# Row factors only in a gated delta rule's preparation, and a norm weight folded into the output weights

## The chip, the cores and the metric

The kernel runs on one core of one Trainium2 chip. The metric is the time of one execution in device microseconds (us); the median of three runs is shown. Engines are named as in the profile: PE is TensorE (matrix products), PEld its weight loads, DVE is VectorE, ACT is ScalarE, POOL is GpSimd, SP is SyncE, whose queue issues most DMAs.

## The reference, cut to what matters

One layer of a decoder trunk on 1040 positions (16 learned meta tokens and 1024 real ones) of width 1024: RMSNorm, one input projection, a gated-DeltaNet group of 4 heads (128 wide) beside a forgetting-attention group of 8 heads (64 wide), one output projection, a SwiGLU feed-forward part, a final norm. The change lies in the DeltaNet group:

```python
q = l2norm(q) * DK ** -0.5;  k = l2norm(k)          # x * rsqrt(sum(x*x) + EPS), per token
gc = cumsum(g)                                       # log decay inside a chunk
a_mat = strict(k @ k.T * exp(gc_i - gc_j) * beta_i)  # strictly lower triangular
u, w = solve(I + a_mat, [v * beta, k * beta * exp(gc)])
# scan over the chunks, with state s:
v_new = u - w @ s
o     = (q * exp(gc)) @ s + (q @ k.T * decay) @ v_new
s     = s * exp(g_last) + (k * exp(g_last - gc)).T @ v_new
# output of the group
o = o * rsqrt(mean(o * o) + EPS) * norm_w * silu(z)
```

`norm_w` (`gdn_norm_w`) has 128 numbers, one per column of a head, the same for all heads. The group's output then meets the rows of `w_out`.

## The kernel before, in words

All large products run in fp32r with three products per pair: each operand is split into a high part (an ACT cast, line 163) and a low part (a DVE difference, line 164). The helper `split` issues both; `load_w` (line 167) loads a block of weights into a raw tile and splits it, in `parts_n[0]` parts.

**First stage** (to about 50 us): for each of 8 blocks of 128 tokens the norm, transposes, and a projection that gives half of the gate z and the decay columns. `gate_out` (line 298) takes silu of z on ACT, multiplies it by the norm weight on POOL (line 302, the weight broadcast to all partitions in `gnw`), and writes it to a record in DRAM, `rec_d`. The other half of z comes later in `fox()`, through the same helper.

**Preparation of the recurrence** (to about 262 us): two pairs of heads. For a pair, k, q and v are projected (`conv_silu`, lines 418 to 429; a causal convolution on DVE), then `gdn_pre` (line 444) runs for each of the two heads. It

- transposes k, squares it and sums (`stat`), does the same for q, and takes the power -1/2 of both on POOL (lines 463 and 464: `rk`, `rq`);
- brings `rk` from a column (one number per token on its partition) into a row that every partition can read: two PE transposes (466, 467), two DVE copies, two DMA writes to `rk_d`, one broadcast read into `rkr` (474);
- loads the row of `gc`, forms the decay `e` and a strictly masked copy `na` (lines 479 to 488; `gcr` and `e` are two halves of one tile `gce`, one exponential for both, two masks on POOL);
- multiplies the products k k^T and k q^T from PSUM (`pq`, line 493) by the decay and the row factors (498, 500), and `na` by the column factor `rkr` on POOL (502);
- writes `na`, the decayed q k^T, k, v, and q to the record (lines 503 to 518), and handles the 16 meta tokens (520 to 526).

The tiles of squares (`sq`) are used again for the transposed values (`vtok`, line 509). `mkv`, the meta tokens' k and v, has two buffers.

`invert_blocks` (line 537) inverts the 32x32 diagonal blocks of `na` on DVE, in a chain of 31 steps of two small instructions (533 and 535). After the second pair, a small inversion of the meta block (`amt`) follows in the same way.

**The merge** (`levels`, line 597, once per pair) puts the inverted blocks together to 64 and 128 on PE. Its loads and copies (601 to 610) come ahead of its first yield, its PE work after it. **The scan** (`chunk`) then runs over 8 chunks, and `fox()` projects the attention group's parts beside both. The out-projection (`wout_block`, `wout_gdn`) starts under the attention.

**What sets the order.** Up to the end of the preparation a planner orders the instructions of every engine by a timeline that it simulates; on the chip each engine then takes its instructions in that order. From `levels` on, the PE order is written out by hand: `PeOrder` counts a time of its own, and chains with due times (`LV0` = 76 and 119 for the two merges) interrupt a filling stream of projections. The other engines stay with the planner. A tile of a pool that is allocated again waits for those that read it; in the pool `ubp` this goes by whole tiles. `issue_after` puts an instruction behind another on the same engine, without a semaphore.

Of the kernel before, what the change touches and what calls it, by code (L numbers as in the profile page):

```python
# [9 lines left out]
F32 = mybir.dt.float32  # L10
# [87 lines left out]
def tile_hymba_layer(ctx, tc, x, meta, attn_norm_w, w_in, conv_w, a_log, dt_bias, gdn_norm_w,  # L98
# [45 lines left out]
    rk_d = dram.tile([GH, T], F32, name="rk_d")  # L144
# [17 lines left out]
    def split(dst_hi, dst_lo, src):  # L162
        cast = nc.scalar.copy(dst_hi, src)  # L163
        tail[0] = (cast, nc.vector.tensor_sub(dst_lo, src, dst_hi.bitcast(F32)))  # L164
        return cast

    def load_w(parts, name, hl=None):
        n = sum(m for _, m in parts)
        raw = wraw.tile([P, WMAX], F32, tag="raw", name=f"raw_{name}")
        o = 0  # L170
        for src, m in parts:
            d = raw[:, o:o + m]
            if len(src.shape) == 3:
                d = d.rearrange("p (k c) -> p k c", k=src.shape[1])
            nc.sync.dma_start(d, src)
            o += m
        hi, lo = hl or (wsp.tile([P, WMAX], F32R, tag=f"w{c}", name=f"w{c}_{name}") for c in ("hi", "lo"))
        for a in range(0, n, n // parts_n[0]):
            b = min(n, a + n // parts_n[0])
            split(hi[:, a:b], lo[:, a:b], raw[:, a:b])  # L180
        return hi, lo
# [114 lines left out]
    gnw = gpool.tile([P, P], F32, name="gnw")  # L296

    def gate_out(t, acc, pool, tag, h0):
        zt = pool.tile([P, 4, 2, DH], F32, tag=tag, name=f"zt{h0}_{t}")
        zt = zt.rearrange("p a b c -> p (a b c)")[:, :256].rearrange("p (h c) -> p h c", h=2)  # L300
        nc.scalar.activation(zt, acc[:, :256].rearrange("p (h c) -> p h c", h=2), AF.Silu)
        nc.gpsimd.tensor_tensor(zt, zt, gnw[:, None, :].broadcast_to([P, 2, P]), op=ALU.mult)
        nc.sync.dma_start(rec_d[t, :, 7, h0:h0 + 2], zt)

    w = None
    for t in range(NT):
        load_norm(t)
        if w is None:
            w = win_block(GZ + 256, 264, "z1")
            nc.sync.dma_start(gnw, gdn_norm_w[0].partition_broadcast(P))  # L310
        acc = proj_tm(t, w, 0, 264, f"z1_{t}")
        nc.vector.tensor_copy(gt[:, t], acc[:, 256:264])
        gate_out(t, acc, zp, "zt", 2)
# [85 lines left out]
    cwr = gp.tile([P, P + NM], F32, tag="rkt", name="cwr")[:48, :P]  # L399
# [14 lines left out]
    rq = gpool.tile([P, GH, NT], F32, name="rq")  # L414
    rk = gpool.tile([P, GH, NS], F32, name="rk")
# [27 lines left out]

    def gdn_pre(h, kq, vt):
# [11 lines left out]
        mkv = gp.tile([NM, 2, P], F32, tag="mkv", bufs=2, name=f"mkv_{h}")  # L456
        nc.scalar.copy(mkv, pt[:NM, 0:2 * P].rearrange("p (a c) -> p a c", a=2))
# [4 lines left out]
        nc.vector.tensor_scalar(stat, stat, EPS, None, op0=ALU.add)
        nc.gpsimd.tensor_tensor(rk[:, h], stat[:, 0:NS], mhalf[:, :NS], op=ALU.pow)
        nc.gpsimd.tensor_tensor(rq[:, h], stat[:, NS:NS + NT], mhalf[:, :NT], op=ALU.pow)
        prk = ps_t(f"prk_{h}")
        nc.tensor.transpose(prk[:NT, :P], rk[:, h, 0:NT], ident)
        nc.tensor.transpose(prk[:1, P:P + NM], rk[:NM, h, NT:NS], ident[:NM, :NM])
        rkt = gp.tile([P, P + NM], F32, tag="rkt", name=f"rkt_{h}")[:NT]
        nc.vector.tensor_copy(rkt[:, :P], prk[:NT, :P])
        nc.vector.tensor_copy(rkt[:1, P:], prk[:1, P:P + NM])  # L470
        nc.sync.dma_start(rk_d[h, NM:T].rearrange("(t c) -> t c", c=P), rkt[:, :P])
        nc.sync.dma_start(rk_d[h:h + 1, 0:NM], rkt[:1, P:])
        rkr = gp.tile([P, T], F32, tag="rkr", name=f"rkr_{h}")
        nc.sync.dma_start(rkr, rk_d[h].partition_broadcast(P))
        nbr = gp.tile([P, NS], F32, tag="nbr", bufs=2, name=f"nbr_{h}")
        nc.vector.tensor_mul(nbr, nbeta[:, :, h], rk[:, h])
        nc.vector.tensor_mul(negc_[:, :, h], negc_[:, :, h], rk[:, h])

        gce = ubp.tile([P, 2, S], F32, tag="ul_p5", name=f"gce_{h}")
        gcr, e = v3(gce[:, 0]), v3(gce[:, 1])  # L480
# [3 lines left out]
        nc.scalar.activation(gce, gce, AF.Exp)  # L484
# [4 lines left out]
        for g in range(4):  # L489
            pq = ps_s(f"pq_{h}_{g}")  # L490
            for i in range(2):
                c = NM + P * (2 * g + i)
                nc.tensor.matmul(pq[:, 256 * i:256 * i + 256], kq[:, 0, c:c + P], kq[:, :, c:c + P],
                                 start=True, stop=True)
            pqv = pq.rearrange("p (i a c) -> p i a c", i=2, a=2)
            for i in range(2):
                t = 2 * g + i
                nc.vector.scalar_tensor_tensor(na[:, t], pqv[:, i, 0], nbr[:, t:t + 1], na[:, t],
                                               op0=ALU.mult, op1=ALU.mult)
                nc.vector.scalar_tensor_tensor(e[:, t], pqv[:, i, 1], rk[:, h, t:t + 1], e[:, t],  # L500
                                               op0=ALU.mult, op1=ALU.mult)
        nc.gpsimd.tensor_tensor(na, na, v3(rkr[:, NM:]), op=ALU.mult)
# [3 lines left out]
        kf = gp.tile([P, NT], F32, tag="kf", name=f"kf_{h}")  # L506
        nc.vector.tensor_mul(kf, rk[:, h, 0:NT], kdec[:, 0:NT, h])
        nc.gpsimd.tensor_tensor(ktok, ktok, kf[:, :, None].broadcast_to([P, NT, P]), op=ALU.mult)
        vtok = v3(sq)
# [12 lines left out]
        nc.vector.tensor_mul(ems[:, h], ems[:, h], rkr[:NM, :NM])  # L522
        nc.vector.scalar_tensor_tensor(nam[:, h], pm[:NM, :NM], nbr[:NM, NT:], ems[:, h], op0=ALU.mult, op1=ALU.mult)
        nc.vector.tensor_mul(kf[:NM, 0:1], rk[:NM, h, NT:NS], kdec[:NM, NT, h:h + 1])
        nc.vector.tensor_scalar(mkv[:, 0], mkv[:, 0], kf[:NM, 0:1], None, op0=ALU.mult)
# [70 lines left out]

    def levels(hp):
# [6 lines left out]
        V.transpose(tb.rearrange("p h t c -> p (h t c)"), ubk.rearrange("p h t c -> p (h t c)"))  # L604
        u = lp.tile([P, 2, NT, P], F32, tag="u", bufs=2, name=f"u_{hp}")
        nc.gpsimd.memset(u, 0.0)
        for b in range(4):
            r = slice(32 * b, 32 * b + 32)
            eng = nc.scalar.copy if b % 2 else V.tensor_copy
            eng(u[r, :, :, r], ubk[r])  # L610
# [41 lines left out]
        def up2_e(i, t0, p2):  # L652
            t2 = lp.tile([64, 2, 4, 64], F32, tag="t2", bufs=2, name=f"t2_{2 * hp + i}_{t0}")
            nc.scalar.copy(t2, p2[lo])
# [7 lines left out]
        def up3_e(i, t0, p3):  # L662
            h, ts = 2 * hp + i, slice(t0, t0 + 4)
            V.tensor_copy(u[lo, i, ts, hi], p3[lo, 0])
# [460 lines left out]
    def wout_block(k0, nb, tiles=None):  # L1125
        ws = ([], [])
        for i in range(2):
            hl = load_w([(wout_w(k0 + 2 * i, nb), 1024)], f"wo{k0}_{nb}{i}", tiles and tiles(i))
            for o, t in zip(ws, hl):
                o.extend(t[:, 512 * k:512 * k + 512] for k in range(2))  # L1130
# [6 lines left out]
    def wout_gdn(nb, tt):  # L1137
        if nb not in wvs:
            parts_n[0] = 2 if nb else 1
            wvs[nb] = wout_block(0, nb)  # L1140
# [547 lines left out]
```

## Time and profile before

| | |
|---|---|
| three runs, median (lowest to highest) | 1315.19 us (1314.64 to 1316.14) |
| profiled execution: time / span from first to last instruction | 1316.6 us / 1314.9 us |
| mean granted PE clock | 0.996 |
| PE / DVE / ACT / POOL busy | 1289.5 / 854.9 / 546.0 / 390.6 us |

A page of the profile gives, for each group of instructions, "line engine operation output<-inputs", its busy time and mean duration, and behind the second bar the idle time of the engine just before it with what ended that idle time. In a time line the brackets at the end of a row hold that idle time for the row alone. In the table of waits the three numbers are the total, the count and the longest. In the chain of waits (the work that ended last, followed back) a row "DMA x<-y" is a transfer that the next step waited for. Matrix products overlap, so PE busy time says where PE stood still rather than how much it does.

### The profile page before, as it was taken

The page shows a single profiled execution, that of the slowest core. Times are in us where ns is not written, and L with a number is a line of the kernel's source. Part 1 is how long each engine was busy: PE and PEld are TensorE (multiplying, and loading weights), DVE is VectorE, ACT ScalarE, POOL GpSimd, SP SyncE. Part 2 cuts the span into 40 slices and gives each one's busy share as a digit, 9 for nine tenths or more (in the row PEclk, how much of TensorE's full clock was granted, in tenths as well). Part 3 has the DMA queues.
Part 4 walks back from the last instruction along what each step waited for, and adds up shares of the span by engine and source line. Part 5 has one row for each costly group of instructions (what it writes and reads, how often), then busy time and mean ns, then how long its engine had stood idle before and what let it go on. Part 6 is the DMA issues. An engine that isn't in the chain of part 4 may idle for free.

```text
span 1314.9 us, 20026 instructions
## 1 busy us (share of the span) xinstructions
PE 1289.5 (98%) x7442; PEld 1128.9 (86%) x7442; DVE 854.9 (65%) x1526; ACT 546.0 (42%) x918; POOL 390.6 (30%) x347
## 2 busy tenths in 40 slices
PE   8999999999999999999999999999999999999998
PEld 8999999898999878887778888888888888888887
DVE  5665779677236768986897765556566565355545
ACT  5543434333223557885553332333323343343332
POOL 2211423601022321113432544554334453020301
PEclk9999999999999999999999999999999999999999
DMA  6331753774469886647434555534454557955523
GB/s 225 102 101 45 204 144 101 215 226 146 157 227 340 223 227 188 169 117 232 170 135 136 183 176 178 173 129 155 155 168 150 176 198 261 405 183 180 211 73 128
DMA packets 184360, 233.88 MB, mean 178 GB/s; under 512 B 19024, under 2 KB 136776, under 8 KB 181448
## 3 DMA queue, kind: packets, MB, share of 16 engines
q1 hardware_dynamic: 181368, 223.97, 52.9%
q0 software_dynamic: 2896, 8.65, 2.3%
q8 instruction: 58, 0.95, 0.3%
q14 instruction: 38, 0.31, 0.1%
HBM read 154.91 MB, written 77.67 MB: 177 GB/s over the span
## 4 chain that ended last, share of the span: by engine, by line
PE 74%; DVE 10%; DMA 7%; ACT 3%; issue 3%; SPq 1%; POOL 1%; POOLq 0%; DVEq 0%; ACTq 0%
PE xp L1569 9%; PE yp L1569 7%; PE gb L1403 5%; PE ud L1403 5%; PE ub L1403 5%; PE gd L1403 5%; PE ua L1403 4%; PE ga L1403 4%; PE pj_fq L207 3%; PE pj_fk L207 2%; PE ue L1403 2%; PE ge L1403 2%; PE wog L207 2%; PE pt L1034 2%; DVE up L533 1%
## 5 line engine op out<-in xcount | busy, mean ns | idle before, releaser
L164 DVE TENSOR_TENSOR al_p<-ra_p,ah_p 128x2048 fp32r<-128x2048 f32 (+1 forms) x21 | 45.7, 2175 | 94.9 <-ACT ah_p L163 94.9
L163 ACT CAST ah_p<-ra_p 128x2048 fp32r<-128x2048 f32 (+1 forms) x21 | 37.1, 1766 | 105.4 <-PE xp L1569 48.5
L1569 PE MATMUL xp<-wh_p,al_p 128*128 128x512 f32 (+1 forms) x176 | 67.3, 382 | 0.0
L1569 PE MATMUL xp<-wl_p,ah_p 128*128 128x512 f32 (+1 forms) x176 | 67.3, 382 | 0.0
L1569 PE MATMUL xp<-wh_p,ah_p 128*128 128x512 f32 (+1 forms) x176 | 67.3, 382 | 0.0
L1456 POOL TENSOR_TENSOR gzw<-gzw,uzt 128x512 f32<-128x512 f32 x11 | 18.4, 1676 | 153.5 <-DVE uzt L1447 127.3
L1456 POOL TENSOR_TENSOR gxy<-gxy,uxy 128x512 f32<-128x512 f32 x22 | 39.0, 1772 | 67.4 <-DVE uxy L1447 59.6
L1403 PE MATMUL gb<-uh_p,w_g_p 128*128 128x512 f32 x176 | 57.8, 389 | 0.0
L1403 PE MATMUL ub<-uh_p,w_u_p 128*128 128x512 f32 x176 | 57.7, 389 | 0.0
L1403 PE MATMUL ud<-uh_p,w_u_p 128*128 128x512 f32 x176 | 57.7, 389 | 0.0
L1403 PE MATMUL gd<-uh_p,w_g_p 128*128 128x512 f32 x176 | 57.7, 389 | 0.0
L164 DVE TENSOR_TENSOR w_u_p<-raw_u,w_u_p 128x512 fp32r<-128x512 f32 x42 | 43.0, 1023 | 21.6 <-ACT w_u_p L163 21.5
L163 ACT CAST ph<-pt 128x512 fp32r<-128x512 f32 (+1 forms) x96 | 45.1, 472 | 26.2 <-PE pt L1034 25.5
L1007 ACT ACTIVATE pr<-pr,sm 128x144 f32<-128x144 f32 (+3 forms) x64 | 50.5, 790 | 7.7 <-DVE sm L1002 7.3
L164 DVE TENSOR_TENSOR pl<-pt,ph 128x512 fp32r<-128x512 f32 (+1 forms) x96 | 51.4, 553 | 3.4 <-ACT ph L163 2.6
L1403 PE MATMUL ga<-uh_p,w_g_p 128*128 128x512 f32 x160 | 52.5, 389 | 0.0
L1403 PE MATMUL ua<-uh_p,w_u_p 128*128 128x512 f32 x160 | 52.5, 389 | 0.0
L1569 PE MATMUL yp<-wh_p,ah_p 128*128 128x512 f32 x132 | 51.3, 389 | 0.0
L1569 PE MATMUL yp<-wl_p,ah_p 128*128 128x512 f32 x132 | 51.3, 389 | 0.0
L1569 PE MATMUL yp<-wh_p,al_p 128*128 128x512 f32 x132 | 51.3, 389 | 0.0
L164 DVE TENSOR_TENSOR wl_p<-rw_p,wh_p 128x2048 fp32r<-128x2048 f32 (+1 forms) x21 | 46.9, 2236 | 3.4 <-ACT wh_p L163 3.4
L163 ACT CAST w_u_p<-raw_u 128x512 fp32r<-128x512 f32 x42 | 26.0, 620 | 53.1 <-PE gd L1403 34.1
(646 smaller groups left out, 4296.7 us busy)
## 6 DMA issues: line engine op xcount, KB each, us to landing
ra_p<-ao_p SPq DMA_DIRECT2D x14, 1024.0 KB
raw_g<-in_w_gate_dram SPq DMA_DIRECT2D x22, 512.0 KB
raw_u<-in_w_up_dram SPq DMA_DIRECT2D x22, 512.0 KB
raw_d<-in_w_down_dram SPq DMA_DIRECT2D x22, 512.0 KB
wt_p<-raw_d SPq DMA_DIRECT2D x33, 256.0 KB
rw_p<-wt_p SPq DMA_DIRECT2D x8, 1024.0 KB
rw_p<-in_w_down_dram SPq DMA_DIRECT2D x6, 1024.0 KB
ao_p<-gzw SPq DMA_DIRECT2D x22, 256.0 KB
```

Of the source, the lines that this page charges most:

```text
L163: cast = nc.scalar.copy(dst_hi, src)
L164: tail[0] = (cast, nc.vector.tensor_sub(dst_lo, src, dst_hi.bitcast(F32)))
L207: nc.tensor.matmul(dst, a, b, start=first, stop=last)
L533: V.tensor_tensor(pr[:, 0:m, 0:i + 1], u[:, 0:m, 0:i + 1], a[:, i:i + 1, 0:i + 1].broadcast_to([u.shape[0], m, i + 1]), op=ALU.mult)
L1007: nc.scalar.activation(pr[:, :n], pr[:, :n], AF.Exp, bias=sm[:, np_ - 1:np_], scale=-1.0, accum_out=rsum[:, h, j:j + 1])
L1034: nc.tensor.transpose(pt[:rows_k, P * j:P * j + P], pts[j][0][:, c0:c0 + rows_k], ident)
L1403: nc.tensor.matmul(dst, a[:, c], b[:, k], start=(first and k == 0 and i == 0), stop=(k == 3 and i == 2), skip_group_check=not first)
L1456: last_mul[0] = G.tensor_tensor(gs[d], gs[d], us[d], op=ALU.mult)
L1569: nc.tensor.matmul(dst[:, n_], a[:, f, c], b[:, f, n_], start=(first and i == 0 and n == 0), stop=(i == NF - 1 and n == 2), skip_group_che ...
```

## The change

The factor of k is taken out of the columns. With the matrix scaled by rows alone, its row factor becomes the square of the old one, that is the reciprocal of `stat` + EPS times -beta (`nbr`), computed on DVE right after k's squares and ahead of q's. The missing factors go elsewhere: `beta` is multiplied by `rk` in place (it is used after the merge, in `ub`), and k's record (`ktok`) and the meta tokens' k are scaled by the decay alone. `rk_d`, the transposes, the copies, the DMAs, `rkr` and `kf` fall away; the powers of k and q become one POOL call on a joint tile `rkq`; the decayed q k^T needs only the decay (four DVE products of 256 columns for eight of 128 with a factor).

Tiles: `gce` is allocated once for all heads, the decay `e` of odd heads gets a tile of its own (`eo`), the values one (`vtk`, which the convolution weights' load uses first), the exponential becomes two. `mkv` has one buffer. The second pair's DVE and ACT copies in `levels` are put behind the last ones of the first pair.

The norm weight no longer multiplies silu(z). It is loaded as one number per partition, and the splits of the output weights' DeltaNet rows are scaled by it: the high part as a scaled copy on ACT, the low part as a fused multiply and subtract on DVE (two blocks of 128 x 1024, then four of 128 x 512).

```diff
@@ -159,12 +158,18 @@
-    def split(dst_hi, dst_lo, src):
-        cast = nc.scalar.copy(dst_hi, src)
-        tail[0] = (cast, nc.vector.tensor_sub(dst_lo, src, dst_hi.bitcast(F32)))
+    def split(dst_hi, dst_lo, src, col=None):
+        if col is None:
+            cast = nc.scalar.copy(dst_hi, src)
+            low = nc.vector.tensor_sub(dst_lo, src, dst_hi.bitcast(F32))
+        else:
+            cast = nc.scalar.activation(dst_hi, src, AF.Copy, scale=col)
+            low = nc.vector.scalar_tensor_tensor(dst_lo, src, col, dst_hi.bitcast(F32),
+                                                 op0=ALU.mult, op1=ALU.subtract)
+        tail[0] = (cast, low)
         return cast
...
@@ -293,13 +298,12 @@
-    gnw = gpool.tile([P, P], F32, name="gnw")
+    gnw = gpool.tile([P, P], F32, name="gnw")[:, 0:1]
...
         nc.scalar.activation(zt, acc[:, :256].rearrange("p (h c) -> p h c", h=2), AF.Silu)
-        nc.gpsimd.tensor_tensor(zt, zt, gnw[:, None, :].broadcast_to([P, 2, P]), op=ALU.mult)
         nc.sync.dma_start(rec_d[t, :, 7, h0:h0 + 2], zt)
...
-            nc.sync.dma_start(gnw, gdn_norm_w[0].partition_broadcast(P))
+            nc.sync.dma_start(gnw, gdn_norm_w.rearrange("o p -> p o"))
...
@@ -411,8 +415,8 @@
-    rq = gpool.tile([P, GH, NT], F32, name="rq")
-    rk = gpool.tile([P, GH, NS], F32, name="rk")
+    rkq = gpool.tile([P, GH, NS + NT], F32, name="rkq")
+    rk, rq = rkq[:, :, 0:NS], rkq[:, :, NS:]
...
+    gce = ubp.tile([P, 2, S], F32, tag="ul_p5", name="gce")
+
     def gdn_pre(h, kq, vt):
...
-        mkv = gp.tile([NM, 2, P], F32, tag="mkv", bufs=2, name=f"mkv_{h}")
+        mkv = gp.tile([NM, 2, P], F32, tag="mkv", name=f"mkv_{h}")
...
+        nc.vector.tensor_scalar(stat[:, 0:NS], stat[:, 0:NS], EPS, None, op0=ALU.add)
+        nbr = gp.tile([P, NS], F32, tag="nbr", bufs=2, name=f"nbr_{h}")
+        nc.vector.reciprocal(nbr, stat[:, 0:NS])
+        nc.vector.tensor_mul(nbr, nbr, nbeta[:, :, h])
         for g, pt in enumerate(tr8(kq[:, 1], f"q{h}")):
             nc.scalar.activation(sqq[:, 512 * g:512 * g + 512], pt, AF.Square)
         nc.vector.tensor_reduce(stat[:, NS:NS + NT], v3(sqq), AX.X, ALU.add)
-        nc.vector.tensor_scalar(stat, stat, EPS, None, op0=ALU.add)
-        nc.gpsimd.tensor_tensor(rk[:, h], stat[:, 0:NS], mhalf[:, :NS], op=ALU.pow)
-        nc.gpsimd.tensor_tensor(rq[:, h], stat[:, NS:NS + NT], mhalf[:, :NT], op=ALU.pow)
-        prk = ps_t(f"prk_{h}")
-        nc.tensor.transpose(prk[:NT, :P], rk[:, h, 0:NT], ident)
-        nc.tensor.transpose(prk[:1, P:P + NM], rk[:NM, h, NT:NS], ident[:NM, :NM])
-        rkt = gp.tile([P, P + NM], F32, tag="rkt", name=f"rkt_{h}")[:NT]
-        nc.vector.tensor_copy(rkt[:, :P], prk[:NT, :P])
-        nc.vector.tensor_copy(rkt[:1, P:], prk[:1, P:P + NM])
-        nc.sync.dma_start(rk_d[h, NM:T].rearrange("(t c) -> t c", c=P), rkt[:, :P])
-        nc.sync.dma_start(rk_d[h:h + 1, 0:NM], rkt[:1, P:])
-        rkr = gp.tile([P, T], F32, tag="rkr", name=f"rkr_{h}")
-        nc.sync.dma_start(rkr, rk_d[h].partition_broadcast(P))
-        nbr = gp.tile([P, NS], F32, tag="nbr", bufs=2, name=f"nbr_{h}")
-        nc.vector.tensor_mul(nbr, nbeta[:, :, h], rk[:, h])
+        nc.vector.tensor_scalar(stat[:, NS:NS + NT], stat[:, NS:NS + NT], EPS, None, op0=ALU.add)
+        nc.gpsimd.tensor_tensor(rkq[:, h], stat[:, 0:NS + NT], mhalf[:, :NS + NT], op=ALU.pow)
         nc.vector.tensor_mul(negc_[:, :, h], negc_[:, :, h], rk[:, h])
-
-        gce = ubp.tile([P, 2, S], F32, tag="ul_p5", name=f"gce_{h}")
-        gcr, e = v3(gce[:, 0]), v3(gce[:, 1])
+        nc.vector.tensor_mul(beta[:, :, h], beta[:, :, h], rk[:, h])
+
+        gcr = v3(gce[:, 0])
+        e = v3(gp.tile([P, S], F32, tag="eo", name=f"e_{h}") if h % 2 else gce[:, 1])
...
-        nc.scalar.activation(gce, gce, AF.Exp)
+        nc.scalar.activation(e, e, AF.Exp)
+        nc.scalar.activation(gcr, gcr, AF.Exp)
...
-                nc.vector.scalar_tensor_tensor(e[:, t], pqv[:, i, 1], rk[:, h, t:t + 1], e[:, t],
-                                               op0=ALU.mult, op1=ALU.mult)
-        nc.gpsimd.tensor_tensor(na, na, v3(rkr[:, NM:]), op=ALU.mult)
+            ts = slice(2 * g, 2 * g + 2)
+            nc.vector.tensor_mul(e[:, ts], pqv[:, :, 1], e[:, ts])
...
-        kf = gp.tile([P, NT], F32, tag="kf", name=f"kf_{h}")
-        nc.vector.tensor_mul(kf, rk[:, h, 0:NT], kdec[:, 0:NT, h])
-        nc.gpsimd.tensor_tensor(ktok, ktok, kf[:, :, None].broadcast_to([P, NT, P]), op=ALU.mult)
-        vtok = v3(sq)
+        nc.gpsimd.tensor_tensor(ktok, ktok, kdec[:, 0:NT, h, None].broadcast_to([P, NT, P]), op=ALU.mult)
+        vtok = v3(gp.tile([P, S], F32, tag="vtk", name=f"vtk_{h}"))
...
-        nc.vector.tensor_mul(ems[:, h], ems[:, h], rkr[:NM, :NM])
...
-        nc.vector.tensor_mul(kf[:NM, 0:1], rk[:NM, h, NT:NS], kdec[:NM, NT, h:h + 1])
-        nc.vector.tensor_scalar(mkv[:, 0], mkv[:, 0], kf[:NM, 0:1], None, op0=ALU.mult)
+        nc.vector.tensor_scalar(mkv[:, 0], mkv[:, 0], kdec[:NM, NT, h:h + 1], None, op0=ALU.mult)
...
@@ -601,13 +597,15 @@ def levels(hp):
-        V.transpose(tb.rearrange("p h t c -> p (h t c)"), ubk.rearrange("p h t c -> p (h t c)"))
+        with tc.issue_after(lv_t["dve"].ins) if hp else nullcontext():
+            V.transpose(tb.rearrange("p h t c -> p (h t c)"), ubk.rearrange("p h t c -> p (h t c)"))
...
-            eng(u[r, :, :, r], ubk[r])
+            with tc.issue_after(lv_t["act" if b % 2 else "dve"].ins) if hp else nullcontext():
+                eng(u[r, :, :, r], ubk[r])
...
-            nc.scalar.copy(t2, p2[lo])
+            lv_t["act"] = nc.scalar.copy(t2, p2[lo])
...
-            V.tensor_copy(u[lo, i, ts, hi], p3[lo, 0])
+            lv_t["dve"] = V.tensor_copy(u[lo, i, ts, hi], p3[lo, 0])
...
-            wvs[nb] = wout_block(0, nb)
+            wvs[nb] = wout_block(0, nb, col=gnw)
```

More of the change, by code (lines that the diff above doesn't have):

```diff
@@ L143, in tile_hymba_layer @@
     gc_d = dram.tile([GH, S], F32, name="gc_d")
-    rk_d = dram.tile([GH, T], F32, name="rk_d")
     rec_d = dram.tile([NT, P, 8, GH, P], F32, name="rec_d")
@@ L160, in tile_hymba_layer, with load_w @@
     tail = [None]
-    def split(dst_hi, dst_lo, src):
-        cast = nc.scalar.copy(dst_hi, src)
-        tail[0] = (cast, nc.vector.tensor_sub(dst_lo, src, dst_hi.bitcast(F32)))
+    def split(dst_hi, dst_lo, src, col=None):
[7 more added lines that the diff above has]
+        tail[0] = (cast, low)
         return cast
-    def load_w(parts, name, hl=None):
+    def load_w(parts, name, hl=None, col=None):
         n = sum(m for _, m in parts)
@@ L179, in load_w @@
             b = min(n, a + n // parts_n[0])
-            split(hi[:, a:b], lo[:, a:b], raw[:, a:b])
+            split(hi[:, a:b], lo[:, a:b], raw[:, a:b], col)
         return hi, lo
@@ L398, in tile_hymba_layer @@
     gp = gpc.enter_context(tc.tile_pool(name="gp", bufs=1))
-    cwr = gp.tile([P, P + NM], F32, tag="rkt", name="cwr")[:48, :P]
+    cwr = gp.tile([P, S], F32, tag="vtk", name="cwr")[:48, :P]
     nc.sync.dma_start(cwr, conv_w.rearrange("i (m p) -> (i m) p", p=P))
@@ L595, in b3 @@
         return col[:, :, None].broadcast_to([col.shape[0], col.shape[1], P])
+    lv_t = {}
     def levels(hp):
@@ L1123, in tile_hymba_layer, with wout_block @@
     wvs = {}
-    def wout_block(k0, nb, tiles=None):
+    def wout_block(k0, nb, tiles=None, col=None):
         ws = ([], [])
         for i in range(2):
-            hl = load_w([(wout_w(k0 + 2 * i, nb), 1024)], f"wo{k0}_{nb}{i}", tiles and tiles(i))
+            hl = load_w([(wout_w(k0 + 2 * i, nb), 1024)], f"wo{k0}_{nb}{i}", tiles and tiles(i), col)
             for o, t in zip(ws, hl):
```

## The prediction

> **What bounds the kernel now.** I read the engine shares first, then the table of 20 us stretches, the waits of TensorE, and last the time lines and the chain of waits around each place where TensorE stood still.
>
> ```profile
> PE 1289.5 (98%) x7442; PEld 1128.9 (86%) x7442; DVE 854.9 (65%) x1526; ACT 546.0 (42%) x918; POOL 390.6 (30%) x347
> ...
> 160.00:180.00 20.00, 19.41 (x120) 18.92 (x119) 13.96 (x24) 7.11 (x9) 4.04 (x4) 1.00 0.77 205
> 180.00:200.00 20.00, 19.38 (x122) 19.10 (x121) 18.93 (x34) 7.27 (x9) 3.84 (x4) 1.00 0.31 90
> ...
> 220.00:240.00 20.00, 18.71 (x144) 16.71 (x142) 18.09 (x35) 8.58 (x15) 7.61 (x7) 1.00 0.68 199
> 240.00:260.00 20.00, 18.74 (x135) 18.10 (x136) 12.24 (x39) 4.61 (x8) 13.30 (x13) 0.91 0.77 210
> ...
> 300.00:320.00 20.00, 18.49 (x270) 16.59 (x269) 15.96 (x44) 5.89 (x11) 1.50 (x4) 1.00 0.52 147
> ```
>
> The columns are the stretch, its length, then the busy time of PE, PEld, DVE, ACT and POOL with counts, the granted clock, and DMA share and GB/s. TensorE is busy 98% of the span, so time taken off another engine is worth nothing by itself. A gain can come only from a TensorE instruction that is gone, from a stretch in which TensorE stood still, or from a stretch at a low clock. The recurrent preparation runs from about 118 to 262 us and its block inversions to about 320; in these rows TensorE idles 0.59 + 0.62 + 1.29 + 1.26 + 1.51 = 5.3 us, and one stretch has a clock of 0.91. The waits say who was late:
>
> ```profile
> PE prk L466 <- POOL rk L463: 2.1, 1, 2.1
> ...
> PE py L644 <- DVE u L634: 0.9, 2, 0.5
> ...
> PE pj_v L197 <- ACT cx_q L423: 0.6, 1, 0.6
> PE pq L493 <- DVE gce L500: 0.6, 1, 0.6
> PE py L644 <- ACT t L654: 0.6, 1, 0.6
> ...
> PE tr_q L437 <- ACT mkv L457: 0.4, 1, 0.4
> ```
>
> The change touches the chain behind every one of these rows.
>
> **The change part by part.**
>
> *The row transposes.* L466 and L467 and everything behind them go: two transposes, two copies, two small writes, one broadcast read and a POOL product per head.
>
> ```profile
> 132.01 0.27 PE L466 MATMUL prk<-ident,rk 128*8 128x128 f32 x1
> ...
> 132.31 1.09 PE L437 MATMUL tr_v<-ident,vt 128*128 128x128 f32 x8
> ...
> 241.26 0.27 PE L466 MATMUL prk<-ident,rk 128*8 128x128 f32 x1 [2.07 <-POOL rk L463]
> ```
>
> From 132.01 to 132.31 the pair takes 0.30 us of TensorE's time; four heads make **1.2 us**. The last row is head 3's pair, which waited 2.07 us for the powers on POOL. No TensorE instruction reads a power any more, so this wait has no successor of its own: **2.1 us**.
>
> *The clock behind that wait.*
>
> ```profile
> 239.00:241.00 2.00, 0.19 (x2) 0.00 (x0) 2.00 (x5) 0.06 (x1) 1.58 (x1) 1.00 0.46 146
> 241.00:242.50 1.50, 1.24 (x11) 1.09 (x11) 1.50 (x6) 1.41 (x1) 1.50 (x2) 1.00 0.51 66
> 242.50:246.00 3.50, 3.50 (x19) 3.26 (x18) 2.92 (x6) 1.71 (x4) 3.50 (x3) 0.53 0.35 47
> ...
> 14.00:17.00 3.00, 1.66 (x13) 1.20 (x11) 2.41 (x4) 1.78 (x6) 1.25 (x2) 1.00 0.71 235
> 17.00:21.00 4.00, 3.28 (x17) 3.13 (x16) 3.37 (x6) 1.74 (x4) 0.55 (x1) 0.57 0.80 264
> ```
>
> TensorE works 0.19 of 2 us from 239, and from 242.5 to 246 it is granted 0.53 of its clock. The other dip, from 17 to 21, also follows a stretch that was half idle (1.66 of 3). I take the dip for the gap's consequence: 3.5 x 0.47 = **1.6 us** that go with it. [...]
>
> *The queue waits of head 3 and of the first inversion.*
>
> ```profile
> 226.59 7.23 DMA rec_d<-gce
> 233.83 3.80 DMA gce<-gc_d
> ...
> 247.98 7.04 DMA rkr<-rk_d
> ...
> 314.05 0.62 ACT u L610
> ...
> 315.32 1.07 ACT t L654 x2
> ```
>
> ```profile
> L619 PE MATMUL py<-u,na x128: 191/191/212, 304.7 to 354.3; 32*32 32x32 f32 x128
> ...
> L502 POOL TENSOR_TENSOR ktna<-ktna,rkr 128x1024 f32<-128x1024 f32 x4 | 11.4, 2862 | 25.3 <-DVE ktna L498 9.9 <-DMA rkr<-rk_d 9.7 <-DVE kst L452 5.6
> ```
>
> In the chain of waits, head 3's decay load stands behind the write of head 2's `gce` (7.23 us), because both halves were one tile; with `e` of odd heads in its own tile that load waits only for the short-lived half. The factor's broadcast (7.04) and its product (2.86 a head) leave the chain altogether, so head 3's matrix reaches the second inversion 9 us earlier or more. TensorE uses that inversion's result only when the second merge starts, and the last products of that kind stand at 354.3, so this is no gain in itself; it takes DVE's inversion of the meta block (`amt`) away from the time of the first merge at 304.7. At 314 the second pair's copies of `ubk` stand in ACT's queue ahead of the first pair's `t`, for which TensorE waits; the change orders them behind it. The `py` waits are 0.9 + 0.6 = 1.5; I take **1.2**, as DVE's copy itself remains.
>
> *The smaller waits.*
>
> ```profile
> 184.12 1.92 ACT L484 ACTIVATE gce<-gce 128x2048 f32<-128x2048 f32 x1
> ...
> 228.62 1.06 ACT L451 ACTIVATE sq<-ktna 128x1024 f32<-128x1024 f32 x1 [4.10 <-DMA rec_d<-sq]
> 229.58 0.34 ACT L457 COPY mkv<-trm 16x256 f32<-16x256 f32 x1
> ```
>
> The copy that TensorE's `pj_v` waited for stood behind one exponential of 1.92 us; it becomes two of about half, the needed one first. `tr_q` waited behind a square that stood 4.10 us for the write of the shared value tile, and values now have their own. With the `pq` wait these are 0.6 + 0.4 + 0.6 = 1.6; the planner will place the copies anew, so I take half, **0.8**.
>
> *New waits.* `mkv` has one buffer, so L457 of heads 1 and 3 waits for the previous head's 16 KB write. Behind it on ACT stand the squares of q and the projection copies, and TensorE's `tr_q` waits for those. The write of head 2 is issued early:
>
> ```profile
> 224.85 1.17 SPq L526 DMA_DIRECT2D mkv_d<-mkv  x1
> ...
> 157.66 3.03 DMA rk_d<-rkt
> ```
>
> It has 4.7 us until L457 at 229.58, where a small write takes 3.03 to land, and it no longer waits for a power but only for the decay. Without that cover it would cost at most the difference, some 3 us. The write of the value tile has much longer. DVE gets a reciprocal, an addition and two products per head, each of at most 128x9 elements; they go into what the eight `e` products of 0.335 us, halved in number (next fence), and the two copies of the transposes leave free.
>
> *Work off the path.* The gate product and the factor's product leave POOL; the products of `e` on DVE become four instead of eight.
>
> ```profile
> L302 POOL TENSOR_TENSOR zt<-zt,gnw 128x256 f32<-128x256 f32 x16 | 15.4, 967 | 23.4 <-ACT zt L301 23.4
> ...
> L500 DVE SCALAR_TENSOR_TENSOR gce<-pq,rk,gce 128x128 f32<-128x128 f32 x32 | 10.6, 335 | 0.7 <-POOL gce L487 0.7
> ...
> 442.59 1.14 ACT L163 CAST whi_wo<-raw_wo 128x512 fp32r<-128x512 f32 x2 [0.55 <-PE pj_fq L207]
> ...
> 181.54 1.23 DVE L483 SCALAR_TENSOR_TENSOR gce<-gce 128x1024 f32<-128x1024 f32 x1
> 182.77 1.23 DVE L164 TENSOR_TENSOR wlo_z<-raw_z,whi_z 128x1024 fp32r<-128x1024 f32 x1
> ```
>
> That is 15.4 us of POOL, with the factor's 11.4 above, at 30% load: worth nothing but the room it gives. Four `e` products of 256 columns lie between 4 and 8 times 0.335 us, so DVE gains 0 to 1.3 us a head, not on TensorE's path. The norm weight moves into six splits of output weights. On DVE the fused form and the plain difference take the same 1.23 us at 128x1024; on ACT a cast of 512 columns takes 0.57. A scaled copy does not stand in the trace; between no difference and doubling it is 0 to 0.57 us a piece, and I take zero, as the squares of that size on ACT (1.06 at 1024 columns, above) cost no more. The new load of the weight, one number a partition, has 400 us.
>
> *The sum.* 1.2 + 2.1 + 1.6 + 1.2 + 0.8 = 6.9. Against it I set 1.0 for waits that a new plan brings: the bounds are zero and 2.1, the longest that the old plan had here, and no row is nearer to one than the other. Net **5.9**. The profiled execution took 1316.6 us around a span of 1314.9; it becomes 1310.7. It stood 1.4 above the median of the three runs, 1315.19, so the median becomes **1309.3**.
>
> **The rivals.** *The waits only move* (no change). If what follows the transposes in TensorE's order was as late as they were, the 2.1 us and the dip stay, and only the transposes and part of the merge come back: 1.2 + 0.7 = 1.9, 1313.3. For it speaks that DVE was busy without a break from 239 to 242.5 and the value transposes stand right behind. Against it: those need only a finished value tile and a free bank, and the wait's row names the power alone.
>
> *The powers in front of the masks* (slower). POOL takes its work in order, and the masks L485 and L487 are what the `pq` products wait for.
>
> ```profile
> 239.41 1.79 POOL L463 TENSOR_TENSOR rk<-kst,mhalf 128x9 f32<-128x9 f32 x1 [4.20 <-DVE kst L462]
> 241.17 2.54 POOL L464 TENSOR_TENSOR rq<-kst,mhalf 128x8 f32<-128x8 f32 x1
> ...
> 247.92 1.09 POOL L485 TENSOR_SCALAR_AFFINE_SELECT ktna<-gce 128x1024 f32<-128x1024 f32 x1
> ```
>
> The powers become one call of about 1.79 + 2.54 = 4.3 us. Since the products no longer wait for a power, the planner may put `pq` earlier; if it counts the power as short, both `sp` banks fill and TensorE stands for power and mask, 4.3 + 1.1 = 5.4 us, and then loses 1.6 by the clock. In heads 1 and 3 that makes 14.0; less the 6.9 gained, the kernel ends at 1322.3. It turns the result from 6.9 us of new idling on. Against it: the same two powers stood ahead of the masks before, and `pq` waited 0.6 us once.
>
> *More than the sum.* If the room on POOL and DVE also shortens the starting stretch and its dip at 17 us (1.7) and the remaining small waits (0.8), and no new wait comes, it is 6.9 + 2.5 = 9.4: 1305.8.
>
> **How the numbers follow.** A difference of 0.2%, 2.6 us, is about what a measurement of this kernel can tell from none. The chances are 0.58 for the forecast, 0.22 for waits that only move, 0.12 for the powers in front of the masks, 0.08 for more. Faster by over 0.2% means below 1312.6: nearly all of the forecast (0.55), all of the last case and a quarter of the moved waits, 0.68. Within 0.2% are the rest of these two, 0.20; slower the third, 0.12. The forecast's own range is 1306.5 to 1312.5: the waits all gone and none new, or half of them gone. With the neighbours it reaches from 1305.0, under the last case, to 1316.5, which leaves out the slower case and little else.
>
> **What would show it.** In the changed profile the rows of `prk`, `rkt` and `rkr` are gone and no row of TensorE's waits names a power. The stretch from 240 to 260 has a clock of 1.00; if TensorE waits there under another name, the second case holds. `gce<-gc_d` no longer follows a write of `gce` by zero, and ACT's `u` copies of the second pair stand behind all `t` copies of the first. A wait of `pq` on POOL's masks above 2 us means the slower case. A wait of ACT's `mkv` on `mkv_d` would make the single buffer wrong. What I cannot see is the new plan as a whole: all rows past 320 us should be as they were, and if they are not, the sum is incomplete.

## The result, and the profile after

The changed kernel takes 1308.06 us (median of 4 runs, 1307.08 to 1308.18) beside 1315.32 us (1314.64 to 1316.14) for the kernel before in the same comparison: a ratio of 0.9941, 95% interval 0.9929 to 0.9954. The forecast was 1309.3. Its profiled execution took 1308.2 us around a span of 1306.5; before these were 1316.6 and 1314.9. The spans differ by 8.4 us, the medians by 7.3.

The stages show where. The next two fences give, for the kernel before and for the changed one, the last product of four kinds. The rows list shortest, median and longest duration in ns, then the first and the last start in us.

```profile
L199 PE MATMUL zg<-whi_z,ul x8: 167/168/169, 46.2 to 47.7; 128*16 128x8 f32 x8
...
L199 PE MATMUL pj_v<-uh,wlo_gv x96: 314/322/326, 94.8 to 201.6; 128*128 128x346 f32 x64, 128*128 128x348 f32 x32
...
L207 PE MATMUL fv<-whi_fv,ul x128: 274/282/425, 242.8 to 294.8; 128*128 128x264 f32 x64, 128*128 128x256 f32 x64
...
L207 PE MATMUL pj_fk<-uh,wlo_fk x96: 315/322/429, 295.2 to 350.1; 128*128 128x346 f32 x64, 128*128 128x348 f32 x32
```

```profile
L204 PE MATMUL zg<-whi_z,ul x8: 167/168/169, 43.6 to 45.0; 128*16 128x8 f32 x8
...
L204 PE MATMUL pj_v<-uh,wlo_gv x96: 315/322/326, 92.1 to 196.4; 128*128 128x346 f32 x64, 128*128 128x348 f32 x32
...
L212 PE MATMUL fv<-whi_fv,ul x128: 274/283/425, 235.7 to 288.9; 128*128 128x264 f32 x64, 128*128 128x256 f32 x64
...
L212 PE MATMUL pj_fk<-uh,wlo_fk x96: 315/322/434, 289.3 to 342.2; 128*128 128x346 f32 x64, 128*128 128x348 f32 x32
```

| stage, up to its last product | before | after | gained so far | in the stage |
|---|---|---|---|---|
| first stage (`zg`) | 47.7 | 45.0 | 2.7 | 2.7 |
| heads 0 and 1 (`pj_v`) | 201.6 | 196.4 | 5.2 | 2.5 |
| heads 2 and 3, value projections (`fv`) | 294.8 | 288.9 | 5.9 | 0.7 |
| both pairs' first part of the merge (`pj_fk`) | 350.1 | 342.2 | 7.9 | 2.0 |
| the rest, to the end of the span | 1314.9 | 1306.5 | 8.4 | 0.5 |

The forecast had nothing for the first row and 3.7 us (2.1 + 1.6) for the third. The table of stretches of the changed kernel, with the columns of the prediction's table, says why the third is small:

```profile
0.00:20.00 20.00, 16.86 (x111) 15.59 (x112) 10.83 (x16) 11.53 (x20) 5.36 (x21) 1.00 0.85 293
...
14.00:17.00 3.00, 1.74 (x14) 1.53 (x15) 2.56 (x5) 1.76 (x3) 0.89 (x1) 1.00 0.69 233
17.00:21.00 4.00, 4.00 (x35) 4.00 (x35) 3.24 (x7) 2.74 (x7) 0.55 (x1) 1.00 0.77 262
...
160.00:180.00 20.00, 20.00 (x128) 20.00 (x127) 16.89 (x40) 7.66 (x12) 0.10 (x1) 1.00 0.43 128
180.00:200.00 20.00, 20.00 (x130) 19.73 (x129) 19.79 (x28) 11.01 (x16) 3.30 (x3) 1.00 0.16 48
...
220.00:240.00 20.00, 20.00 (x160) 19.07 (x159) 6.85 (x19) 3.52 (x6) 6.76 (x8) 1.00 0.85 214
240.00:260.00 20.00, 17.00 (x127) 16.82 (x126) 14.54 (x60) 3.73 (x9) 1.28 (x2) 0.91 0.84 237
...
300.00:320.00 20.00, 20.00 (x231) 18.72 (x232) 8.24 (x13) 7.43 (x13) 4.30 (x4) 1.00 0.33 108
```

Of the five stretches of the prediction's table in which TensorE idled, four are now full. The fifth is worse: from 240 to 260 TensorE stands for 3.0 us, and the clock is 0.91 as before. In the waits of TensorE no row names a power any more, but a new row heads the list:

```profile
PE fv L212 <- DVE up L527: 3.0, 1, 3.0
```

It lies between the products that start at 241.14 and 244.43, within a value projection (`fv`) of the attention group. The time lines of ACT, DVE and SP in the changed kernel show the chain behind it, one fence each (a row SPq is the issue of a DMA in SP's queue):

```profile
241.33 0.36 ACT L163 CAST fvt_-1_2741<-fv_-1_2716 16x256 fp32r<-16x256 f32 x1 [7.23 <-DMA rec_d<-zt]
```

```profile
242.32 0.71 DVE L601 STREAM_TRANSPOSE tb<-ubk 128x512 f32<-128x512 f32 x1 [6.97 <-DMA ubk<-ud_d]
...
243.79 0.41 DVE L164 TENSOR_TENSOR fvt_-1_2741<-fv_-1_2716,fvt_-1_2741 16x256 fp32r<-16x256 f32 x1
```

```profile
229.70 1.92 SPq L502 DMA_DIRECT2D ad_d<-ktna  x4
231.66 0.45 SPq L509 DMA_DIRECT2D rec_d<-ktna  x1
232.21 0.53 SPq L510 DMA_DIRECT2D rec_d<-e  x1
232.96 2.58 SPq L537 DMA_DIRECT2D ad<-ad_d  x2
235.58 1.13 SPq L307 DMA_DIRECT2D rec_d<-zt  x2
237.56 0.32 SPq L597 DMA_DIRECT2D ubk<-ud_d  x1
...
240.50 2.70 SPq L599 DMA_DIRECT2D na<-rec_d  x2
```

The split of the first value block frees the PSUM bank that TensorE needs; the wait's row names `up` only because the inversion's first product starts right behind it on DVE, at 244.21. The cast of that split needs a tile slot that a gate tile held until its record write landed; its difference on DVE stands behind copies that waited for `ubk`. Both transfers had stood in SP's queue behind head 3's matrix (`ad_d`, `rec_d<-ktna`, `ad`).

### The profile page after: what moved, and what is told of

The parts are those of the page before. It is cut to its first block, busy times and chain, and to the rows that moved or that the text cites. A ratio compares the mean times of both kernels' runs of the same rounds, so it can differ in the third digit from the quotient of the medians.

```text
span 1306.5 us, 19943 instructions
## 1 busy us (share of the span) xinstructions
PE 1284.0 (98%) x7434; PEld 1127.0 (86%) x7434; DVE 847.0 (65%) x1502; ACT 549.3 (42%) x924; POOL 360.5 (28%) x323
## 4 chain that ended last, share of the span: by engine, by line
PE 85%; DVE 6%; ACT 3%; DMA 3%; issue 2%; SPq 1%; POOL 0%; POOLq 0%; DVEq 0%; ACTq 0%
PE xp L1567 9%; PE yp L1567 7%; PE gb L1401 5%; PE ud L1401 5%; PE gd L1401 5%; PE ub L1401 5%; PE ua L1401 4%; PE ga L1401 4%; PE pj_fk L212 4%; PE pj_fq L212 3%; PE fv L212 3%; PE ue L1401 2%; PE ge L1401 2%; PE pt L1032 2%; PE wog L212 2%
## 5 line engine op out<-in xcount | busy, mean ns | idle before, releaser
L164 DVE TENSOR_TENSOR al_p<-ra_p,ah_p 128x2048 fp32r<-128x2048 f32 (+1 forms) x21 | 46.7, 2222 | 94.5 <-ACT ah_p L163 94.5
L164 DVE TENSOR_TENSOR w_u_p<-raw_u,w_u_p 128x512 fp32r<-128x512 f32 x42 | 42.9, 1022 | 21.7 <-ACT w_u_p L163 21.5
L1454 POOL TENSOR_TENSOR gxy<-gxy,uxy 128x512 f32<-128x512 f32 x22 | 38.9, 1768 | 65.3 <-DVE uxy L1445 54.3
```

The lines of the kernel that those rows point to most:

```text
L164: low = nc.vector.tensor_sub(dst_lo, src, dst_hi.bitcast(F32))
L1454: last_mul[0] = G.tensor_tensor(gs[d], gs[d], us[d], op=ALU.mult)
```

## The experiments

Each comparison has its own runs of the kernel before on its chip; their medians were 1315.3 for the changed kernel and 1317.5 to 1318.0 for the runs below, so ratios are given beside times. The changed kernel was not run again beside them; mult_back and no_order, whose edits touch nothing that TensorE waits for in the changed kernel, came to 1308.2 and 1308.8, so on their chips the times bear a comparison with 1308.1 to within 1 us. Times of one stage come from the profiles, one of each kernel.

### The two halves apart: norm_only, rows_only

```diff
# norm_only: the kernel before with the norm weight moved: one column loaded, no product on POOL, scaled splits
...
+            cast = nc.scalar.activation(dst_hi, src, AF.Copy, scale=col)
...
-        nc.gpsimd.tensor_tensor(zt, zt, gnw[:, None, :].broadcast_to([P, 2, P]), op=ALU.mult)
...
# rows_only: the changed kernel with all of this undone
```

> The kernel before with only the norm weight moved (one column loaded, no product on POOL, scaled splits of the output weights); the recurrent preparation is the old one. Theory A, the start belongs to the norm weight: the first stage ends 2.7 us earlier than before and has no dip of the clock at 17 us, the wait of TensorE for the power at 240 us stays (2.1 us), total 1315.3 - 2.7 = 1312.6. Theory B, the forecast's (room on POOL, worth nothing): the first stage as before, 1315.3.

> The changed kernel without the move of the norm weight (broadcast load, product on POOL and plain splits again). Theory A: the start as before with its dip at 17 us, the rest as in the changed kernel, 1308.1 + 2.7 = 1310.8. Theory B (the start's gain comes from elsewhere, the order of the loads or the tiles): the start as in the changed kernel, 1308.1.

norm_only takes 1321.6 us beside 1317.5, a ratio of 1.0027 (1.0014 to 1.0041): slower. rows_only takes 1313.1, 0.9967 (0.9954 to 0.9980). The start goes the way that theory A says, though not to its end: the first stage of norm_only ends at 45.3, that of rows_only at 46.7 (47.7 was expected), and both have a half clock from 10.9 to 14.3 and none at 17. The totals do not follow, 1321.6 for 1312.6 expected and 1313.1 for 1310.8: the norm weight's move costs 4.1 us where the rest is old, and saves 1313.1 - 1308.1 = 5.0 where it is new (by the ratios 3.6 and 3.4). The parts don't add. In norm_only heads 0 to 3 give back more than the start gained (`pj_v` waits 1.5 instead of 0.6, and the power's wait is 3.2 instead of 2.1), and then the merge loses. Its ACT and PE time lines and its stretches:

```profile
316.47 0.58 ACT L659 COPY t<-py 64x512 f32<-64x512 f32 x1 [4.38 <-PE py L654]
319.18 1.24 ACT L615 COPY u<-ubk 32x512 f32<-32x512 f32 x2 [2.13 <-DMA ubk<-ud_d]
320.45 0.58 ACT L659 COPY t<-py 64x512 f32<-64x512 f32 x1
```

```profile
321.08 0.41 PE L649 MATMUL py<-ident,u 64*64 64x64 f32 x4 [2.04 <-ACT t L659]
```

```profile
318.13:321.54 3.41, 1.36 (x16) 0.90 (x16) 2.28 (x7) 1.81 (x3) 0.00 (x0) 1.00 0.22 74
321.54:324.96 3.42, 3.42 (x38) 3.30 (x39) 2.98 (x9) 1.59 (x3) 1.82 (x2) 0.50 0.00 0
```

The planner put the second pair's `u` copies between two `t` copies of the first pair. They waited for their load until 319.18, TensorE stood 2.04 us, and 3.4 us at half clock followed. In rows_only the wait of `fv` is 5.6 us instead of 3.0, with two stretches of 3.4 us at half clock behind it; that profile's execution took 1315.5 us, 2.4 above the median of its kernel, so this is more than the usual loss.

### The start: load_back, mult_back

```diff
# load_back
+            nc.sync.dma_start(gnwf[:, 1:], gdn_norm_w[0, 1:].partition_broadcast(P))
# mult_back
...
+        if h0:
+            nc.gpsimd.tensor_tensor(zt, zt, ones[:, None, :].broadcast_to([P, 2, P]), op=ALU.mult)
```

> The changed kernel with 127 columns of the broadcast norm weight (63.5 KB) loaded again at the old place, read by nobody, and no product. Theory A1, the transfer holds up the second block of tokens: its square on ACT waits for the DMA again, the first stage ends up to 2.7 us later, 1310.8. Theory A2, the product on POOL was the cause: start as in the changed kernel, 1308.1.

> The changed kernel with the eight products on POOL back in the first stage, by a tile of ones that is there already, and no broadcast load. Theory A1 (the transfer): start as in the changed kernel, 1308.1. [...]

load_back takes 1311.0 us (ratio 0.9945, 0.9925 to 0.9966), mult_back 1308.2 (0.9924, 0.9899 to 0.9948). The first stage ends at 48.8 with the load and at 45.3 with the products, so it is the transfer. All 14 profiles agree: the first stage ends at 46.7, 47.7 and 48.8 in the three kernels with the broadcast load (rows_only, before, load_back) and between 45.0 and 45.3 in the eleven without it. The time lines of ACT, of the kernel before, the changed one and load_back in turn, show the square of the second block of tokens:

```profile
11.99 1.06 ACT L251 ACTIVATE jk_a<-xt 128x1024 f32<-128x1024 f32 x1 [0.68 <-DMA xt<-in_x_dram]
```

```profile
10.89 1.08 ACT L256 ACTIVATE jk_a<-xt 128x1024 f32<-128x1024 f32 x1
```

```profile
13.91 1.06 ACT L256 ACTIVATE jk_a<-xt 128x1024 f32<-128x1024 f32 x1 [3.07 <-DMA xt<-in_x_dram]
```

The 63.5 KB stand in front of 512 KB blocks on DMA engines that are 0.85 busy in the first 20 us of the changed kernel, and later blocks shift: the one that SP issues at 9.62 there is issued at 12.71 in load_back. That load_back is even later than the kernel before (48.8 against 47.7) is left open.

### The new gap: own_z, late_u0, late_own, late_ld

```diff
# own_z: two slots for the gate tiles, two for the value tiles, instead of three for both
...
-            gate_out(t, acc, fvp, "fvt", 0)
+            gate_out(t, acc, fvp, "fzt", 0)
# late_u0: DVE and ACT copies of the first pair behind the last split issued before them; late_own: both
...
+        with tc.issue_after((lv_t["dve"] if hp else tail[0][1]).ins):
# late_ld: late_u0's copies behind the tenth value split, and the loads behind the fifth value record
...
+        with tc.issue_after(fvs[4][2].ins) if not hp else nullcontext():
             nc.sync.dma_start(ubk, ud_d[hp].rearrange("b j h t k -> (b j) h t k"))
...
```

> The changed kernel with the gate tiles of the attention group's stream in two slots of their own (256 columns each) and two instead of three slots for the value tiles; TensorE's order is the same. Theory S, the slot: the value tile's cast on ACT waited 7.23 us for the record write of an earlier gate tile, so the gap of 3.0 us at 241 and the half clock behind it (1.7) go: 1308.1 - 4.7 = 1303.4. Theory Q, the queue of DVE: the difference that frees the bank stands behind copies that wait for the inverted blocks until 242.3, so the gap stays at 2.5 us or more: 1308.

> The changed kernel with the first pair's DVE and ACT copies of inverted blocks in the merge put behind the last split that was issued before them; TensorE's order is the same. Theory Q: the gap at 241 shrinks to the wait for the slot, which ends at 241.3, that is to 0.5 or less, and the half clock goes: 1308.1 - 4.2 = 1303.9. Theory S: the gap stays at 2 us or more and the total within 1 us of 1308.1. If both causes stand in line, the gap shrinks to some 0.5 to 1 here and by less than 1 with the slot alone.

> Both edits. Every theory: no gap at 241 and no half clock behind it, 1308.1 - 4.7 = 1303.4. If TensorE then waits elsewhere by the same 3 us, the wait only moved again.

> The changed kernel with the first pair's loads for the merge (inverted blocks and matrix) put in SP's queue behind the fifth value record, and the copies that use them behind the tenth value split. Theory SP, the queue that issues the DMAs is what is late between 228 and 248 (the value records wait behind those loads, which wait for the second pair's records): no gap of TensorE above 1 us from 237 to 256, no half clock there, 1308.1 - 4.5 = 1303.6. Theory of a moving wait: TensorE stands 2 to 3.5 us at another place of the stretch, 1308 or more.

own_z takes 1311.8 (ratio 0.9953, 0.9938 to 0.9968), late_u0 1308.7 (0.9928, 0.9905 to 0.9952), late_own 1311.6 (0.9956, 0.9942 to 0.9970), late_ld 1304.9 (0.9893, 0.9868 to 0.9918). Neither S nor Q holds for the total: each edit removes the wait that it was made for, and TensorE stands elsewhere, in own_z first for the gate tiles, which have two slots now, and in both at 253. The time lines of PE, first own_z, then late_u0:

```profile
240.69 0.39 PE L212 MATMUL fv<-whi_fv,uh 128*128 128x264 f32 x1 [2.12 <-ACT zt L306]
...
253.57 0.36 PE L212 MATMUL fv<-whi_fv,uh 128*128 128x264 f32 x1 [2.31 <-DVE fr L932]
```

```profile
253.69 0.36 PE L212 MATMUL fv<-whi_fv,uh 128*128 128x264 f32 x1 [3.46 <-DVE fr L932]
```

At 253 the splits wait for slots whose value records (`v_d`) SP issues only from 246.2 on (246.4 in late_u0), behind the loads of `na`. With those loads moved behind the fifth value record (late_ld) the largest wait left in the stretch is 1.1 us and the clock stays at 1.00. Moving the copies alone, though not as far (late_u0), brought nothing, so it is the order in SP's queue, as theory SP says, and 3.2 of the expected 4.5 us come back.

### The order in the merge: no_order, norm_order

```diff
# no_order: undone in the changed kernel; norm_order: added to norm_only
-        with tc.issue_after(lv_t["dve"].ins) if hp else nullcontext():
...
-            with tc.issue_after(lv_t["act" if b % 2 else "dve"].ins) if hp else nullcontext():
```

> The changed kernel without the order that puts the second pair's DVE and ACT copies in the merge behind those of the first pair; TensorE's order is the same. Forecast's theory: the waits of the products py for ACT's t and DVE's u come back, 0.7 to 1.5 us, and the total is 1308.1 + 1.2 = 1309.3. Rival: the copies would not stand in front anyway in the changed plan, 1308.1.

> The kernel before with the norm weight moved, and with the order of the second pair's copies in the merge. Theory: what made the norm weight's move alone slower is for the greater part the merge, where ACT's copies of the second pair, waiting for their load until 319, stood between the first pair's copies (waits of py 2.0 and 1.7, then a half clock of 1.7): these go and the total falls by some 4 to 5 from 1321.6 to 1317. Rival: the loss lies in the preparation (the power waited for longer, 3.2, and twice a half clock) and the order saves under 1.5 us.

no_order takes 1308.8 us (0.9929, 0.9906 to 0.9952), the changed kernel's time: the rival holds. norm_order takes 1318.0 (1.0003, 0.9986 to 1.0020), 3.6 less than norm_only, though the two intervals overlap; its profile has lost the 2.04 us and the half clock, and the other waits went from 1.7 down to 0.8. From the last `fv` to the last `pj_fk` it takes 54.3 us, where norm_only took 59.0. So the order works where the second pair is late, and is idle here, because the second pair isn't late. The issues of the second pair's load (last start), in the kernel before, the changed one and norm_order:

```profile
L601 SPq DMA_DIRECT2D ubk<-ud_d x2: 344/424/503, 267.0 to 311.2; - x2
```

```profile
L597 SPq DMA_DIRECT2D ubk<-ud_d x2: 320/334/348, 237.6 to 282.2; - x2
```

```profile
L608 SPq DMA_DIRECT2D ubk<-ud_d x2: 338/341/344, 265.6 to 314.0; - x2
```

All profiles divide in this way: in the eleven kernels that issue this load at 289 us or earlier the stage from the last `fv` to the last `pj_fk` takes 53.3 us, in the three that issue it at 311 or later 54.3 to 59.0.

### The own tiles: tiles_shared, decay_shared

```diff
# decay_shared
-        e = v3(gp.tile([P, S], F32, tag="eo", name=f"e_{h}") if h % 2 else gce[:, 1])
+        e = v3(gce[:, 1])
# tiles_shared: this, and
-        vtok = v3(gp.tile([P, S], F32, tag="vtk", name=f"vtk_{h}"))
+        vtok = v3(sq)
```

> The changed kernel without the own tiles: the decay of all heads in the joint tile, the transposed values in the tile of squares. The forecast's theory: the decay's load of heads 1 and 3 waits for the record write again and arrives some 4 us later, with waits of TensorE of 0.8 to 1.6 us in heads 1 and 3 and nothing more: 1309.3. Rival, the tiles carry the most of the gain: the masks are late for pq, which stands over 2 us with a half clock behind it: 1312 or more.

> The changed kernel without the own tile for the decay of odd heads alone; the values keep theirs. With both tiles shared there was no gap of TensorE in the stretch from 237 to 256 and the total was 3 us lower. Theory E, the decay's tile: it brought head 3's matrix some 7 us earlier to SP's queue, in front of the gate and value records; with it shared again the gap is gone, 1308.1 - 3.3 = 1304.8. Theory V, the values' tile was the cause: the gap of 3 us and its half clock stay, 1308.

Both beat the changed kernel: tiles_shared 1305.0 us (0.9895, 0.9870 to 0.9919), decay_shared 1304.3 (0.9900, 0.9882 to 0.9918). Neither expectation for tiles_shared holds; of those for decay_shared, theory E does. In both, heads 0 and 1 end 0.1 us from where they end in the changed kernel (196.5 and 196.4), so the own tiles brought nothing there; in heads 2 and 3 the decay's tile costs 3.4 (the last `fv` at 285.5 instead of 288.9). SP's queue in decay_shared:

```profile
228.74 4.38 SPq L307 DMA_DIRECT2D rec_d<-zt  x3
...
236.67 1.82 SPq L502 DMA_DIRECT2D ad_d<-ktna  x4
...
243.71 0.59 SPq L929 DMA_DIRECT2D v_d<-fvt_-1_2739  x1
...
244.81 0.55 SPq L597 DMA_DIRECT2D ubk<-ud_d  x1
245.41 4.56 SPq L599 DMA_DIRECT2D na<-rec_d  x3
```

Head 3's matrix reaches the queue at 236.67 instead of 229.70. The gate records are now in front of it, and the first value records in front of the loads of `ubk` and `na`; TensorE stands for 0.5 us in all. The stretch from 237 to 256, in the changed kernel and then in decay_shared:

```profile
237.00:256.00 19.00, 16.00 (x119) 15.82 (x118) 10.75 (x48) 3.36 (x8) 3.66 (x3) 0.91 0.96 271
```

```profile
237.00:256.00 19.00, 18.47 (x151) 18.29 (x151) 7.19 (x34) 2.73 (x6) 3.48 (x3) 1.00 1.03 279
```

The load of the second inversion's result is issued at 288.6 instead of 282.2, still ahead of the merge. decay_shared and late_ld differ by 0.6 us and their intervals overlap; which is better stays open, and both together were not tried.

## Why the prediction was right, and where it was not

The number came out by luck: the parts were off on both sides, and the errors cancelled.

**The transposes, 1.2 us.** They are gone, and with them 8 instructions of TensorE (7442 before). Their share was not measured apart. The engine shares of the changed kernel:

```profile
PE 1284.0 (98%) x7434; PEld 1127.0 (86%) x7434; DVE 847.0 (65%) x1502; ACT 549.3 (42%) x924; POOL 360.5 (28%) x323
```

**The wait for the power and the clock behind it, 2.1 + 1.6, and the 1.0 against the sum.** Heads 2 and 3 gained 0.7 us in all, since in the changed kernel another wait, of 3.0 us, stands 2 us later with a half clock behind it. By the test that the prediction gave, the second case holds for this place, but its mechanism doesn't. In decay_shared, which differs only in the decay's tile, the old wait is gone and no new one of its size came: there heads 2 and 3 gain 93.2 - 89.0 = 4.2 us, near the 0.6 + 2.1 + 1.6 = 4.3 of two pairs of transposes, the power and the clock. So "this wait has no successor of its own" is borne out, and the step that failed is the term for new waits. The line "so this is no gain in itself" put the earlier matrix at nothing, and the matrix, ready earlier, was issued in front of what TensorE needed next (229.70 instead of 236.67 in SP's queue), which cost 3.4 us (decay_shared). I had looked for waits among what reads the power, and not in SP's queue, which the earlier matrix fills earlier. The bound of 2.1 for that term, the longest wait of the old plan, was too small: the new wait is 3.0 and brings its own stretch at half clock.

**The first merge, 1.2.** Mis-sized: it gained 2.0, and the stretch from 300 to 320 is full. The cause was not the order of the copies (no_order), but the second pair's blocks, 29 us earlier by the issue of their load, and 22.6 us earlier without the decay's own tile (288.6 in decay_shared). "9 us earlier or more" was right, and it was to be put into this sum.

**The smaller waits, 0.8.** All three are gone; heads 0 and 1 gained 2.5, of which the idle time of 160 to 200 in the prediction's table is 0.6 + 0.6 and the two pairs of transposes 0.6. The other 0.7 I can't place. The values' own tile, to which the wait of `tr_q` was credited, is not the reason: tiles_shared does without it and has no such wait either.

**The start, 0.** "Worth nothing but the room it gives" was right for POOL's products (mult_back) and missed what goes with them: the broadcast load, 2.7 us. The prediction priced the new load and not the removed one. The third rival had the dip at 17 us in it, 1.7, and put it down to room on POOL and DVE, which is not what gave it.

**The norm weight at the split.** The prediction took no difference for a scaled cast of 512 columns on ACT. It takes 0.716 us where the plain one took 0.616 in the kernel before; the prediction's 0.57 was half of a row of 1.14 us in which two casts overlap. The joint power takes 3.06 us instead of the 4.3 forecast; neither shows in a wait of TensorE.

```profile
L166 ACT ACTIVATE whi_wo<-raw_wo,gnw x4: 709/716/728, 434.7 to 437.7; 128x512 fp32r<-128x512 f32 x4
```

```profile
L473 POOL TENSOR_TENSOR rkq<-kst,mhalf x4: 3058/3059/3070, 125.1 to 221.5; 128x17 f32<-128x17 f32 x4
```

**The slower case** did not come: no wait of TensorE names POOL's masks. The single buffer of `mkv` did no harm either: ACT's `mkv` copies show no wait for a write.

In sum: forecast 6.9 - 1.0. Measured by stage, 2.7 at the start instead of 0; 2.5 + 0.7 in the heads instead of the 5.7 of transposes, power, clock and smaller waits, less 1.0; 2.0 in the merge instead of 1.2; 0.5 later, where single waits differ from profile to profile and no run was made to separate them.

## What to carry to other kernels

When a change makes something ready earlier, look for what it now stands in front of in the queues that the whole region shares, here the one that issues the DMAs: head 3's matrix was issued 7.0 us earlier than in decay_shared, what TensorE needed next stood behind it, and the last `fv` came 3.4 us later. A transfer that is removed counts as much as one that is added: the one removed here had 64 KB, in a stretch in which the DMAs of the changed kernel are 0.85 busy, and the first stage ended 2.7 us earlier without it. Parts of a change to a planned kernel are to be timed together and apart: here one part made the kernel 4.1 us slower alone and 5.0 faster with the other.

## What the runs showed of the hardware

The granted clock changed on a grid of 3.413 us: up to 1290 us the kernel before has two stretches at half clock, each 3.41 us long, which start at 17.45 and 242.73 us, 225.28 us or 66 such steps apart. The length of a gap alone did not say whether it cost a half clock: one of 2.07 us did in the kernel before, one of 2.8 us in load_back did not. The stretches of that grid around the gap of 3.0 us, in the changed kernel:

```profile
242.10:245.51 3.41, 1.08 (x9) 1.12 (x10) 2.97 (x12) 1.88 (x4) 0.00 (x0) 1.00 1.06 306
245.51:248.92 3.41, 3.41 (x17) 3.41 (x17) 3.03 (x18) 0.00 (x0) 0.00 (x0) 0.50 1.15 303
```

and in load_back, whose gap at 245.28 was 2.8 us long:

```profile
243.58:246.99 3.41, 1.70 (x14) 1.49 (x13) 0.98 (x2) 1.44 (x3) 1.35 (x2) 1.00 1.01 296
246.99:250.40 3.41, 2.29 (x19) 2.32 (x20) 3.02 (x18) 0.80 (x3) 0.00 (x0) 1.00 1.14 315
...
373.29:376.70 3.41, 3.41 (x25) 2.77 (x25) 0.52 (x1) 0.85 (x3) 0.00 (x0) 1.00 0.85 257
376.70:380.11 3.41, 3.41 (x14) 3.41 (x15) 1.28 (x1) 1.72 (x2) 1.04 (x1) 0.50 1.00 300
```

That gap fell on two windows, 0.50 and 0.67 busy, and cost no clock. By a count over the 14 profiles, every window of the grid in which TensorE was busy 0.45 or less (14 windows) was followed by one at half clock; of those from 0.50 to 0.62 busy, 5 of 14 were (one of the two at 0.53), all five in the first 15 us; of the fuller ones up to 1290 us, one at 1.00 was, the row from 373.29 above, and two that were themselves at half clock. The gap of 2.07 us in the kernel before left TensorE 0.43 busy in the window from 239.31 (1.47 of 3.42), with 0.50 of the clock in the next. The least idle time among the 14 windows was about 1.9 us (1.55 busy of 3.42 from 251.82 in late_u0).

Why a half clock followed the full window from 373.29 was not shown. Its time line in load_back has sixteen products that use 16 of the 128 rows. They fill 0.63 of it, and the other products 0.44. In the other 13 profiles the same sixteen products fill at most 0.58 of a window and the others at least 0.48 (0.34 and 0.70 in the changed kernel, from 371.80), and no half clock follows. This is one case, and no run was made to test whether the sixteen were the cause.

```profile
373.25 1.04 PE L779 MATMUL pvm<-mkv,ubm 16*16 16x128 f32 x8
...
375.50 1.15 PE L786 MATMUL pdm<-vnm,mkv 16*128 16x128 f32 x8
```

A broadcast load of some 64 KB early in the first stage moved its end by 1.4 us (norm_only against rows_only) to 3.8 us (the changed kernel against load_back). At the 293 GB/s of the first 20 us its bytes would take 0.2 us, by an estimate. Some 1.7 of the 3.8 us are a half clock from 18.3 to 21.7 in load_back that the changed kernel doesn't have.
